# Probabilities of one attention head turned by DMA in 16-bit planes, and its products with V three slots later

## The chip, the cores and the metric

One core of a Trainium2 chip. The metric is the device time of one execution in microseconds. Engines are named as in the profile: PE is TensorE (PEld its weight loads), DVE is VectorE, ACT is ScalarE, POOL is GpSimd, SP is SyncE, which here only issues DMAs. L639 is line 639 of the kernel before.

## The reference

One encoder layer over 512 tokens of width 2048: a projection, two attention mixers of 8 heads each, an output projection, and a gated feed-forward part. The change is in the second mixer ("B"), which in the kernel is one masked softmax a head:

```
sc  = einsum('nbqhd,nbkhd->nbhqk', qb, kwin)
sc  = where(valid, sc, -inf)            # three dilated windows, merged by their denominators
lse = logsumexp(sc);  p = exp(sc - lse)
o   = einsum('nbhqk,nbkhd->nbqhd', p, vwin)
...
mixed = concatenate([rmsnorm(A), rmsnorm(B)]);  x = x + einsum('bse,ed->bsd', mixed, w_out)
```

## The kernel before, in words

**Products.** Every fp32 product is three passes (`mm3`, L229 to L231): both operands are split into a high part, written by ACT, and the remainder, written by DVE (`split`, L220 and L221). So each operand that a matmul takes has passed ACT and then DVE.

**Order.** All work is issued by one Python loop over weight units. A unit of the output projection is 12 matmuls of 128x512 (four row blocks, three passes each). Between units, and in the middle of most, a share of the side queue is issued: `give` pops tasks until its credit is used up. `drain_until` pops tasks until something is there that the next unit needs; reloading a parked head's output (`Back.load`, "oback") drains until that head's `oT` has been issued. The order on each engine is fixed when the program is built, and each engine takes its instructions in that order.

**Attention slots.** `head_slot(s)` issues what is due in slot s. A head has four blocks of 128 queries, so 16 heads take 64 slots and some more. In this document **slot 0 is the first score block of head B5**, the sixth head of the second kind; B5's scores are in slots 0 to 3, those of B6 in 4 to 7, those of B7 in 8 to 11. In its slots a block goes through:

- the score (`mm3`) into a PSUM bank, and at once the mask and row maximum on DVE (L639, an instruction that the profile calls CUSTOM_DVE_ANT_0, writing `p`), then the exponential on ACT (L649);
- one slot later the division by the row sum on DVE (L653, L654);
- `pt` (`TURN_LAG` = 5 slots after the first score): four PE transposes (L659) of one 128-column block of the four `p` tiles into a PSUM bank, then split into `pTh` (ACT) and `pTl` (DVE);
- `pv` (`VALUE_LAG` = 6): the product with V, three matmuls on `pTh`, `pTl`, `pTh`; after the last block `fin` copies the sum out (`oT`) and squares it.

**Turning by DMA.** q and k of later heads are already turned without PE, by the class `Turned`: `part` writes the low and the high 16 bits of the fp32 words as two planes ("plane", ACT, L551), `turn` transposes them by DMA ("words", SP, L556), `merge` interleaves them again ("merged", ACT, L561). The result is split like any operand (L220 to L224).

**Neighbours.** In the same stretch ACT and DVE split the weights ("arena" or "w" from "raw", L302 and L307), the reloaded outputs ("arena" from "oback", L1171 and L1175) and V of the next head ("arena" from "vraw"), and DVE adds finished banks of the output projection to x (L1195). PE can reuse those banks only after L1195.

Of the kernel before, what the change touches and what calls it, by code (L numbers as in the profile page):

```python
# [24 lines left out]
NT = S // P  # L25
# [37 lines left out]
TURN_LAG = 5  # L63
HEADS_HELD = 4
ROWS_AT = (6, 8, 10, 12, 14, 16, 19, 22, 25, 28)
VALUE_LAG = 6
COLUMN_BLOCKS = 3
SUM_LEAD = 6
ATTEND_PAST = 4
TURNED_ON_PE = {"A": 2, "B": 4}  # L70


def f32(ap):
    return ap.bitcast(F32)
# [3 lines left out]
def encoder_block(ctx, tc, x, w_in, g_q_a, g_k_a, w_out, w_gate_up, w_down, g_final, x_t, gains, c_ident, c_mask,  # L78
# [11 lines left out]
    def nm(base):  # L90
        counter[0] += 1
        return f"{base}_{counter[0]}"

    def slot(base, dtype=F32, shape=(P, 512)):
        return sp.tile(list(shape), dtype, tag="s", name=nm(base))
# [19 lines left out]
    def small(n=4):  # L115
        used[0] += n
        assert used[0] <= 512
        return fixed[:, used[0] - n:used[0]]
# [47 lines left out]
    def place(m, i):  # L166
        return form_tile(m, i).rearrange("p a b -> p (a b)")
# [46 lines left out]
    def split(src, name, gain=None, at=None):  # L214
        if at is None:
            hi, lo = slot(name + "h", F32R), slot(name + "l", F32R)
        else:
            hi, lo = (place(*h) for h in at)
        if gain is None:
            nc.scalar.activation(hi, src, AF.Copy)  # L220
            nc.vector.tensor_tensor(lo, src, f32(hi), op=OP.subtract)  # L221
        else:
            nc.scalar.activation(hi, src, AF.Copy, scale=gain)
            nc.vector.scalar_tensor_tensor(lo, src, gain, f32(hi), op0=OP.mult, op1=OP.subtract)  # L224
        return hi, lo
# [13 lines left out]
    class Pair:  # L239
        def __init__(self):  # L240
            self.parts = [sp.tile([P, 512], F32R, tag="tw", bufs=2 * TWINS, name=nm("tw")) for _ in range(2)]

        def __getitem__(self, at):
            return self.parts[at[1]]
# [252 lines left out]
    def reload(name, dst):  # L497
        assert stored[name] == NT, name
        whole = slot(name, F32, (P, NT, 512))
        nc.sync.dma_start(whole, spill[name].rearrange("t p c -> p t c"))  # L500
        dst.update((t, whole[:, t]) for t in range(NT))
        dst["whole"] = whole
# [68 lines left out]
    heads = []  # L571
    of_head = [small(12) for _ in range(HEADS_HELD)]

    class Head:
        def __init__(self, kind, h):
            self.kind, self.h = kind, h
            self.p, self.o = {}, None
            self.negm, self.z, self.rz = None, None, None

        def by_dma(self):  # L580
            return self.h >= TURNED_ON_PE[self.kind]

# [118 lines left out]
    def head_at(slot):  # L701
        h, i = divmod(slot, NT)
        return (heads[h], i) if 0 <= h < len(heads) else (None, i)

    def head_slot(s):
        def at(lag, f, only=None):
            head, i = head_at(s - lag)
            if head and (only is None or i == only):
                f(head, i)
        at(VALUE_LAG + 1, lambda head, i: head.add_squares(), NT - 1)  # L710
        at(0, Head.score)
        at(1, Head.norm)
        at(TURN_LAG, Head.pt)
        at(0, Head.exp)
        at(VALUE_LAG, Head.pv)
        at(VALUE_LAG, lambda head, i: head.fin(), NT - 1)

        def begin(lag, kind, f, dma=True):
            at(lag, lambda head, i: f(head) if head.kind == kind and head.by_dma() == dma else None, 0)
        begin(-4, "A", Head.tq, False)  # L720
        begin(-4, "B", Head.tq, False)
        for kind in "AB":
            begin(-2, kind, Head.tk, False)
        begin(-2, "A", Head.split_q)
        begin(-2, "A", Head.split_k)
        begin(-3, "A", Head.merge_q)
        begin(-3, "B", Head.split_q)
        begin(-4, "B", Head.merge_q)
        begin(-2, "B", Head.split_k)
        begin(-3, "B", Head.merge_k)  # L730
# [5 lines left out]
    def light(cost, tasks):  # L736
        return [weighed(cost, f) for f in tasks]

    def attention_tasks():
# [20 lines left out]
        def at(slot, tasks):  # L760
            extra.setdefault(slot, []).extend(tasks)
# [12 lines left out]
        for j in range(4):  # L774
            s = NT * (NHA + 2 * j)
            if 2 * j < TURNED_ON_PE["B"]:
                at(s - 11, light(0.1, [lambda j=j: reload(f"qkB{j}", qkB[j])]))
# [10 lines left out]
        for s in range(2 * NHA * NT + VALUE_LAG + 2):  # L788
            cost = 1.5 if s < NHA * NT else 1.2 if s < 2 * NHA * NT else 0.7
            todo += [weighed(cost, lambda s=s: head_slot(s))] + extra.get(s, [])  # L790
# [474 lines left out]
    for kind in "AB":  # L1265
        for c in range(NC):
            out_chunk(kind, c)
        if kind == "A":
            attend.append(len(units) + ATTEND_PAST)
    attend[1] += ATTEND_PAST  # L1270

# [279 lines left out]
    at = [0.0]  # L1551
# [147 lines left out]
```

## Time and profile before

| | |
|---|---|
| time, median of 3 runs | 1949.36 us (1949.17 to 1949.64) |
| the profiled execution's own time | 1947.76 us |
| its span, first to last instruction | 1946.0 us |
| busy share of the span | PE 99%, PEld 82%, DVE 79%, ACT 59%, POOL 7% |
| DMA | 413.50 MB, mean 212 GB/s |

The span is what the trace covers; 1.76 us of the execution lie around it. A busy share is a mean over stages; the stretch of the change runs from about 536 to 600 us.

### The profile page before, as it was taken

To read this page: it belongs to the slowest core of one execution; us is meant where nothing else is said; L and a number is where in the kernel's file an instruction comes from. 1 tells how busy PE (TensorE), PEld (TensorE's weight loads), DVE (VectorE), ACT (ScalarE), POOL (GpSimd) and SP (SyncE) were. 2 spreads that over 40 slices of the span, in tenths; PEclk is the share of its full clock that TensorE was granted. 3 is DMA by queue.
4 is the path that set the end of the run, shared out by engine and by line. 5 is a ranking of instruction groups with operands and counts; after the bars stand their busy time and mean duration, and the time that the engine had idled before them with its cause. 6 is when DMAs were issued, how large, how long until landed. Compare 5 with 4: busy or idle time off the path is not lost.

```text
span 1946.0 us, 24535 instructions
## 1 busy us (share of the span) xinstructions
PE 1932.1 (99%) x8687; PEld 1593.4 (82%) x8687; DVE 1537.4 (79%) x2020; ACT 1152.7 (59%) x1673; POOL 140.6 (7%) x184
## 2 busy tenths in 40 slices
PE   9999999999999999999999999999999999999998
PEld 7888887888888888888888888888888888888886
DVE  7987768888785697778778778787788978787886
ACT  7755556675765565555555555555555666555555
POOL 1000011000000000000000000000000121111121
PEclk9999999999999999999999999999999999999999
DMA  9676694354442556858658768678587798868865
GB/s 347 235 263 225 216 290 118 92 184 146 124 147 98 174 196 204 284 144 286 241 164 284 225 195 285 196 231 296 145 283 269 215 243 266 230 162 243 239 146 168
DMA packets 268924, 413.50 MB, mean 212 GB/s; under 512 B 75584, under 2 KB 102720, under 8 KB 268672
## 3 DMA queue, kind: packets, MB, share of 16 engines
q1 hardware_dynamic: 237968, 325.31, 51.6%
q0 software_dynamic: 22480, 60.57, 12.4%
q10 hardware_dynamic: 8352, 26.05, 4.1%
q8 instruction: 68, 1.11, 0.2%
q14 instruction: 56, 0.46, 0.1%
HBM read 334.52 MB, written 62.65 MB: 204 GB/s over the span
## 4 chain that ended last, share of the span: by engine, by line
PE 94%; DVE 3%; ACT 2%; issue 1%; DMA 0%; ACTq 0%; DVEq 0%; POOLq 0%; POOL 0%; SPq 0%
PE b L229 31%; PE b L231 30%; PE b L230 30%; PE b L659 1%; ACT rj L448 0%; DVE x L1195 0%; PE b L1241 0%; DVE w L307 0%; DVE ra L461 0%; ACT w L302 0%; DVE tw L966 0%; DVE qA L464 0%; DVE qA L470 0%; DMA stage<-in_w_in_dram 0%; DVE fixed L635 0%
## 5 line engine op out<-in xcount | busy, mean ns | idle before, releaser
L907 ACT ACTIVATE wide<-raw 128x1024 fp32r<-128x1024 f32 x462 | 487.1, 1058 | 457.6 <-PE b L231 269.6
L910 DVE TENSOR_TENSOR wide<-raw,wide 128x1024 fp32r<-128x1024 f32 x462 | 562.8, 1223 | 202.8 <-ACT wide L907 191.5
L229 PE MATMUL b<-wide,arena 128*128 128x512 f32 x1848 | 719.8, 390 | 0.0
L231 PE MATMUL b<-wide,arena 128*128 128x512 f32 x1848 | 719.2, 389 | 0.0
L230 PE MATMUL b<-wide,arena 128*128 128x512 f32 x1848 | 719.1, 389 | 0.0
L231 PEld LDWEIGHTS b<-wide,arena 128*128 128x128 f32 x1848 | 346.9, 188 | 72.3
L230 PEld LDWEIGHTS b<-wide,arena 128*128 128x128 f32 x1848 | 346.9, 188 | 71.7
L229 PEld LDWEIGHTS b<-wide,arena 128*128 128x128 f32 x1848 | 346.9, 188 | 71.7
L1043 DVE TENSOR_TENSOR raw<-raw,raw 128x1024 f32<-128x1024 f32 x264 | 321.6, 1220 | 7.0 <-DMA raw<-in_w_gate_up_dram 7.0
L230 PE MATMUL b<-tw,arena 128*128 128x512 f32 x396 | 154.3, 390 | 0.6 <-DVE tw L966 0.6
L231 PE MATMUL b<-tw,arena 128*128 128x512 f32 x396 | 154.2, 389 | 0.0
L229 PE MATMUL b<-tw,arena 128*128 128x512 f32 x396 | 154.1, 389 | 0.0
L963 ACT ACTIVATE tw<-stage 128x512 fp32r<-128x512 f32 x140 | 85.5, 629 | 69.3 <-DVE stage L1043 45.9
L966 DVE TENSOR_TENSOR tw<-stage,tw 128x512 fp32r<-128x512 f32 x140 | 93.9, 688 | 22.1 <-ACT tw L963 15.9
L229 PE MATMUL b<-w,arena 128*128 128x512 f32 x240 | 95.2, 397 | 0.0
L231 PE MATMUL b<-w,arena 128*128 128x512 f32 x240 | 93.9, 391 | 0.0
L230 PE MATMUL b<-w,arena 128*128 128x512 f32 x240 | 93.5, 390 | 0.0
L230 PEld LDWEIGHTS b<-tw,arena 128*128 128x128 f32 x396 | 74.3, 188 | 16.7 <-DVE tw L966 1.4
L231 PEld LDWEIGHTS b<-tw,arena 128*128 128x128 f32 x396 | 74.3, 188 | 15.9 <-DVE arena L354 0.4
L229 PEld LDWEIGHTS b<-tw,arena 128*128 128x128 f32 x396 | 74.3, 188 | 15.5
L380 DVE TENSOR_TENSOR pair<-pair 128x256 f32<-128x256 f32 x120 | 46.4, 423 | 46.7 <-ACT pair L1244 23.2
L220 ACT ACTIVATE pTh<-b 128x512 fp32r<-128x512 f32 x64 | 38.3, 598 | 64.4 <-PE b L659 62.5
(243 smaller groups left out, 2118.1 us busy)
## 6 DMA issues: line engine op xcount, KB each, us to landing
raw<-in_w_gate_up_dram SPq DMA_DIRECT2D x308, 512.0 KB, 6.3
raw<-in_w_down_dram SPq DMA_DIRECT2D x88, 512.0 KB, 7.4
stage<-in_w_in_dram SPq DMA_DIRECT2D x111, 256.0 KB, 5.4
forms<-pair POOLq DMA_DIRECT2D x22, 896.0 KB, 6.3
fr<-forms ACTq DMA_DIRECT2D x35, 512.0 KB, 5.3
raw<-in_w_out_dram SPq DMA_DIRECT2D x32, 512.0 KB, 4.2
x1d<-s POOLq DMA_DIRECT2D x54, 256.0 KB, 6.5
stage<-in_w_in_dram SPq DMA_DIRECT2D x90, 128.0 KB, 3.6
```

Source lines behind the costliest of these rows:

```text
L220: nc.scalar.activation(hi, src, AF.Copy)
L229: nc.tensor.matmul(dst, ah, bh, start=start, stop=False, skip_group_check=chained)
L230: nc.tensor.matmul(dst, ah, bl, start=False, stop=False, skip_group_check=chained)
L231: nc.tensor.matmul(dst, al, bh, start=False, stop=stop, skip_group_check=chained)
L380: nc.vector.tensor_tensor(out, x, y, op=op)
L659: nc.tensor.transpose(ps[:, t * P:(t + 1) * P], self.p[t][:, kb * P:(kb + 1) * P], ident)
L907: nc.scalar.activation(self.hi, self.src, AF.Copy)
L910: nc.vector.tensor_tensor(self.lo, self.src, f32(self.hi), op=OP.subtract)
L963: nc.scalar.activation(self.pair[:, 0], self.src, AF.Copy)
L966: nc.vector.tensor_tensor(self.pair[:, 1], self.src, f32(self.pair[:, 0]), op=OP.subtract)
L1043: nc.vector.tensor_tensor(t[dst], t[src[0]], t[src[1]], op=OP.add if form == "m6" else OP.subtract)
```

## The change

The probabilities of head B5 alone go through the DMA transpose: their planes are written in slots 2 to 5 and turned in slots 3 to 6, merged and split in slots 8 to 11, and multiplied with V in slots 9 to 12 (before: transposed in slots 5 to 8, multiplied in slots 6 to 9). `fin` and the sum of squares of B5 move from slots 9 and 10 to 12 and 13. Lines of the kernel after are 2 higher up to the class `Turned` and 24 to 31 higher below it: L221 becomes L223, L551 L553, L561 L563, L639 L663, L1195 L1226.

```diff
+P_BY_DMA = (('B', 5),)
+P_LAG = 3
...
+    class Rows:
+        def __init__(self, tiles):
+            self.tiles = tiles
+
+        def __getitem__(self, at):
+            return self.tiles.pop(at[1])
+
...
+        def p_by_dma(self):
+            return (self.kind, self.h) in P_BY_DMA
+
+        def p_part(self, t):
+            if t == 0:
+                self.turned_p = Turned(lambda: Rows(self.p))
+            self.turned_p.part(t)
+
+        def p_turn(self, t):
+            self.turned_p.turn(t)
+
+        def p_merge(self, kb):
+            self.pTs = getattr(self, "pTs", {})
+            self.pTs[kb] = split(self.turned_p.merge(kb), "pT")
...
-        at(VALUE_LAG + 1, lambda head, i: head.add_squares(), NT - 1)
+        def either(lag, f, dma, only=None):
+            at(lag, lambda head, i: f(head, i) if head.p_by_dma() == dma else None, only)
+        for late, dma in ((P_LAG, True), (0, False)):
+            either(VALUE_LAG + late + 1, lambda head, i: head.add_squares(), dma, NT - 1)
         at(0, Head.score)
         at(1, Head.norm)
-        at(TURN_LAG, Head.pt)
+        either(TURN_LAG, Head.pt, False)
         at(0, Head.exp)
-        at(VALUE_LAG, Head.pv)
-        at(VALUE_LAG, lambda head, i: head.fin(), NT - 1)
+        either(2, Head.p_part, True)
+        either(3, Head.p_turn, True)
+        either(TURN_LAG + P_LAG, Head.p_merge, True)
+        for late, dma in ((P_LAG, True), (0, False)):
+            either(VALUE_LAG + late, Head.pv, dma)
+            either(VALUE_LAG + late, lambda head, i: head.fin(), dma, NT - 1)
```

**ACT, slot 2.** Before; `p_4754` is B5's third exponential, `merged_4738` is k of head B6, whose high part goes to the arena:

```order
L220 ACTIVATE pTh_4762<-b_76 128x512
L649 ACTIVATE p_4754,fixed<-p_4754,fixed 128x512
L220 ACTIVATE arena_85<-merged_4738 128x512
L302 ACTIVATE arena_84<-raw_4496 128x512
L220 ACTIVATE pTh_4806<-b_75 128x512
```

The same place now:

```order
L222 ACTIVATE pTh_4762<-b_76 128x512
L673 ACTIVATE p_4754,fixed<-p_4754,fixed 128x512
L553 ACTIVATE plane_4767<-p_4670 128x1024
L222 ACTIVATE arena_85<-merged_4738 128x512
L304 ACTIVATE arena_84<-raw_4496 128x512
L222 ACTIVATE pTh_4808<-b_75 128x512
```

The first plane of B5's probabilities stands ahead of the high part of k.

**DVE, from the division in slot 9 to the mask of slot 10.** Before; `x_403` is x of the output projection:

```order
L654 TENSOR_SCALAR p_4994<-p_4994,fixed 128x512
L221 TENSOR_TENSOR pTl_5052<-b_75,pTh_5051 128x512
L307 TENSOR_TENSOR w_5023<-raw_4740,w_5022 128x512
L1175 SCALAR_TENSOR_TENSOR arena_85<-oback_4978,fixed,arena_85 128x512
L1195 SCALAR_TENSOR_TENSOR x_403_4784<-b_71,fixed,x_403_4784 128x512
L1195 SCALAR_TENSOR_TENSOR x_403_4784<-b_77,fixed,x_403_4784 128x512
L688 TENSOR_TENSOR acc_4217<-acc_4217,sq_5062 128x512
L639 ISA p_5092,fixed<-b_74,mask 128x512
```

And now:

```order
L678 TENSOR_SCALAR p_4977<-p_4977,fixed 128x512
L223 TENSOR_TENSOR pTl_5030<-b_73,pTh_5029 128x512
L223 TENSOR_TENSOR pTl_5037<-merged_5034,pTh_5036 128x512
L309 TENSOR_TENSOR w_5001<-raw_4740,w_5000 128x512
L1206 SCALAR_TENSOR_TENSOR arena_85<-oback_4961,fixed,arena_85 128x512
L1226 SCALAR_TENSOR_TENSOR x_404_4786<-b_71,fixed,x_404_4786 128x512
L1226 SCALAR_TENSOR_TENSOR x_404_4786<-b_77,fixed,x_404_4786 128x512
L663 ISA p_5070,fixed<-b_75,mask 128x512
```

The remainder of the merged block of B5 (`pTl_5037`) is new and stands ahead of four other instructions and of the next mask. ACT's order in the same slot of the kernel after shows what that remainder waits for (`p_5021` is the exponential of slot 9, whose mask is one slot up in DVE's order):

```order
L222 ACTIVATE pTh_5029<-b_73 128x512
L673 ACTIVATE p_5021,fixed<-p_5021,fixed 128x512
L563 ACTIVATE merged_5034<-words_4815 128x1024
L222 ACTIVATE pTh_5036<-merged_5034 128x512
L304 ACTIVATE w_5049<-raw_4826 128x512
```

The merge and its high part come behind the exponential of the same slot.

**PE, from the last transpose of slot 11 to slot 12.** Before; `b_78` is the bank of B6's output, `w` are weight units:

```order
L659 MATMUL b_74<-fixed,p_4960 128x128
L229 MATMUL b_78<-pTh_5100,arena_85 128x512
L230 MATMUL b_78<-pTl_5101,arena_85 128x512
L231 MATMUL b_78<-pTh_5100,arena_85 128x512
L229 MATMUL b_76<-w_5022,arena_85 128x512
L230 MATMUL b_76<-w_5023,arena_85 128x512
L231 MATMUL b_76<-w_5022,arena_85 128x512
L229 MATMUL b_75<-w_5022,arena_85 128x512
L230 MATMUL b_75<-w_5023,arena_85 128x512
L231 MATMUL b_75<-w_5022,arena_85 128x512
L659 MATMUL b_72<-fixed,p_4833 128x128
L659 MATMUL b_72<-fixed,p_4876 128x128
```

Now, with `b_76` the bank of B5's output and `b_78` that of B6's:

```order
L683 MATMUL b_72<-fixed,p_4954 128x128
L231 MATMUL b_76<-pTh_5085,arena_85 128x512
L232 MATMUL b_76<-pTl_5086,arena_85 128x512
L233 MATMUL b_76<-pTh_5085,arena_85 128x512
L231 MATMUL b_78<-pTh_5078,arena_85 128x512
L232 MATMUL b_78<-pTl_5079,arena_85 128x512
L233 MATMUL b_78<-pTh_5078,arena_85 128x512
L683 MATMUL b_75<-fixed,p_4839 128x128
L683 MATMUL b_75<-fixed,p_4885 128x128
L683 MATMUL b_75<-fixed,p_4925 128x128
L683 MATMUL b_75<-fixed,p_4954 128x128
L231 MATMUL b_76<-pTh_5135,arena_85 128x512
```

Slot 12 follows slot 11 with no weight matmul between: the reload of B5's output drains the side queue until B5's `fin`, which is now in slot 12. In slots 10 to 12 the products of B5 stand ahead of those of B6.

## Rows read from the trace of the kernel before

**Rows 1.** The page: the chain that ended last, share of the span by engine.

```profile
PE 94%; DVE 3%; ACT 2%; issue 1%; DMA 0%; ACTq 0%; DVEq 0%; POOLq 0%; POOL 0%; SPq 0%
```

**Rows 2.** Busy time from 563 to 581 us: PE, PEld, DVE, ACT, POOL, PEclk.

```profile
563.00:581.00 18.00, 18.00 (x89) 14.86 (x88) 16.20 (x36) 11.69 (x24) 0.54 (x1) 1.00 0.38 128
```

**Rows 3.** All waits of PE from 520 to 600 us: total, times, longest.

```profile
PE b L659 <- DVE x L1195: 0.6, 1, 0.6
```

**Rows 4.** Timeline of PE around slot 10: start, us, engine, line.

```profile
572.70 0.39 PE L231 MATMUL b<-arena 128*128 128x512 f32 x1
572.93 0.60 PE L659 MATMUL b<-fixed,p 128*128 128x128 f32 x4
...
574.07 0.40 PE L229 MATMUL b<-w,arena 128*128 128x512 f32 x1
...
576.82 0.39 PE L229 MATMUL b<-arena 128*128 128x512 f32 x1
```

**Rows 5.** The chain that ended last, in slots 2 and 3: start, us, what.

```profile
537.61 0.53 ACT arena L220
...
538.77 0.76 DVE x L1195
...
539.58 0.66 PE b L659 x4
```

**Rows 6.** Timeline of ACT with a merge and a plane of q and k.

```profile
515.20 1.18 ACT L561 ACTIVATE merged<-words 128x1024 uint16<-128x1024 uint16 x1
516.27 1.06 ACT L551 ACTIVATE plane<-qkB 128x1024 uint16<-128x1024 uint16 x1
517.22 0.63 ACT L302 ACTIVATE arena<-raw 128x512 fp32r<-128x512 f32 x1
```

**Rows 7.** All that writes or reads "words": duration ns min/median/max; last row the DMAs.

```profile
L556 SPq DMA_TRANSPOSE words<-plane x16: 1232/1250/2371, 323.0 to 517.4; - x16
...
DMA to landing us min/median/max: 3.0/3.1/6.1
```

**Rows 8.** All that writes or reads "merged": DVE's remainder of k.

```profile
L221 DVE TENSOR_TENSOR arena<-merged,arena x4: 692/693/693, 500.5 to 557.5; 128x512 fp32r<-128x512 f32 x4
```

**Rows 9.** Timeline of DVE in slot 5, up to the mask of slot 6.

```profile
550.32 0.69 DVE L639 CUSTOM_DVE_ANT_0 p<-b,mask 128x512 f32<-128x512 f32 x1 [1.28 <-PE b L231]
...
551.53 0.69 DVE L221 TENSOR_TENSOR pTl<-b,pTh 128x512 fp32r<-128x512 f32 x1
553.58 0.69 DVE L224 SCALAR_TENSOR_TENSOR arena<-merged,arena 128x512 fp32r<-128x512 f32 x1 [1.36 <-ACT arena L223]
...
555.39 0.68 DVE L639 CUSTOM_DVE_ANT_0 p<-b,mask 128x512 f32<-128x512 f32 x1
```

**Rows 10.** Timeline of ACT in slots 5 and 6.

```profile
551.25 0.71 ACT L649 ACTIVATE p<-p,fixed 128x512 f32<-128x512 f32 x1
...
556.12 0.73 ACT L649 ACTIVATE p<-p,fixed 128x512 f32<-128x512 f32 x1 [0.21 <-DVE fixed L639]
...
556.84 0.61 ACT L220 ACTIVATE arena<-merged 128x512 fp32r<-128x512 f32 x1
```

**Rows 11.** Timeline of DVE in slot 8, up to the mask of slot 9.

```profile
562.64 0.69 DVE L639 CUSTOM_DVE_ANT_0 p<-b,mask 128x512 f32<-128x512 f32 x1 [0.70 <-PE b L231]
...
565.54 0.69 DVE L307 TENSOR_TENSOR w<-raw,w 128x512 fp32r<-128x512 f32 x1
566.14 0.75 DVE L1175 SCALAR_TENSOR_TENSOR arena<-oback,fixed,arena 128x512 fp32r<-128x512 f32 x1
566.80 0.75 DVE L1195 SCALAR_TENSOR_TENSOR x<-b,fixed,x 128x512 f32<-128x512 f32 x1
...
568.57 0.69 DVE L639 CUSTOM_DVE_ANT_0 p<-b,mask 128x512 f32<-128x512 f32 x1
```

**Rows 12.** DMA issues: tiles, queue, operation, count, KB each, us to landing.

```profile
oB<-oT POOLq DMA_DIRECT2D x6, 256.0 KB, 2.6
oback<-oB SPq DMA_DIRECT2D x6, 256.0 KB, 3.0
```

## The prediction

> **What bounds the kernel now.** I read the page first. The chain that ended last is 94% PE [rows 1], so a stretch is worth what it adds to or takes from PE. Then the list of PE's waits around the change: from 520 to 600 us there is one, 0.6 us, for DVE's L1195 [rows 3]. In the second half of that stretch PE is busy for 18.00 of 18 us at clock 1.00, DVE for 16.20 and ACT for 11.69 [rows 2]: DVE has 10% left, ACT 35%. So PE has no slack; whatever DVE hands over late is paid in full. Last I read the timelines, to see in what order ACT and DVE hand over. The reader is to see there that both engines take their queues in order: a DVE row in slot 5 stands idle for 1.36 us for a high part that ACT has not yet written, and what is queued behind it stands with it [rows 9].
>
> **Removed.** Sixteen PE transposes. A group of four starts 0.23 us after the last score matmul, and the first weight matmul, behind three product matmuls, 1.14 us after the group, of which the three take 0.69 at 0.229 each (12 matmuls are 2.75) [rows 4]: a group costs 0.45 us, four groups 1.8 us. All of it is on PE's path. The twelve product matmuls only move.
>
> The Trainium skill, page "VectorE: DVE Perf Modes", section "The three transpose paths", prices one 128x128 bf16 transpose at 390 ns on TensorE and 1309 ns through the DMA crossbar, and its table of rules takes TensorE wherever a PSUM destination is good enough. By that figure, 16 transposes would give back an estimated 6.2 us and the sum below would be +1.5; the row says 1.8, since transposes follow each other in a pipeline, and I take the row.
>
> **Added on ACT.** Four planes: 0.95 us each from start to next start. Four merges: 1.07 us each [rows 6]. The four high parts stay, now read from SBUF as k's is, 0.61 us each [rows 10]. That is 8.1 us more over slots 2 to 11, some 40 us in which ACT idles for about a third [rows 2]; the sum fits, so the question is only where it stands in the queue.
>
> **Added on DMA.** Four transposes on SP, 1.25 us to issue (2.37 at most) and 3.1 us to landing (6.1 at most) [rows 7]. The last plane is written in slot 5 and first read in slot 8, and the masks of these slots start 12 us apart [rows 9, 11], so I cost them at nothing; what hides them is the three slots of lag, and with a lag of one they would be on the path. The loads behind them on SP (V of B6, the first reloaded output) are issued in slot 6 instead of earlier and read in slots 7 and 8, with 3.0 us to landing [rows 12]; I cost them at nothing too.
>
> **Slot 3, sure loss.** The one wait of PE in this stretch comes from a chain without slack: ACT's high part of B6's k at 537.61, DVE's remainder, L1195 at 538.77, then PE at 539.58 [rows 5]. The first plane now stands directly ahead of that high part. It delays all of it by 0.95 us, and PE is already waiting: **+0.95 us**.
>
> **Slots 5 to 8, lateness builds up.** With that 0.95 the mask of slot 5 starts at 551.27. Its exponential starts 0.73 later, at 552.00, where it was 551.25 before [rows 9, 10]; then comes the last plane, 0.95, then as before `oT`, the square and the high part of q. So DVE gets that high part at 555.28, not 553.58: 1.70 later. It waits for it in order, and the mask of slot 6 moves from 555.39 to 557.09 [rows 9]. From there: exponential 557.82 and 0.72 long, high part of k 558.54 and 0.61 long [rows 10], so DVE at 559.17, its remainder and a weight remainder 0.60 each, mask of slot 7 at 560.4; with 1.21 for mask and division [rows 9] and another remainder, mask of slot 8 at 562.2. PE finishes that score sooner than before: 562.6 before [rows 11], + 0.95, less three groups (1.35) and two moved products (six matmuls, 1.38), 560.8. So this mask starts 1.4 us late. Nothing on PE waits for it yet.
>
> **Slots 8 to 12, the loop.** Each of these slots has a ring through the two queues that was not there before. The mask releases the exponential; the merge stands behind the exponential on ACT; the high part follows the merge; DVE's new remainder waits for that high part and stands ahead of the next mask. Before, the high part came from a PE transpose ahead of the exponential, so the ring was open. One turn is 0.73 + 0.72 + 1.07 + 0.64 + 0.60 = 3.8 us (the 0.60 is DVE's pitch for the remainder, 0.69 long), plus what stands between remainder and mask on DVE: a weight remainder 0.60, an output remainder 0.66, and in two of the three slots two L1195 of together 1.4 (0.75 each, overlapping), in one also V's remainder, 0.60 [rows 6, 8, 10, 11]. That makes 7.0 (slot 8 to 9), 6.4 (9 to 10), 5.0 us (10 to 11). From the mask of slot 11 to the end of the last remainder of B5 it is another 3.9 (0.73, 0.72, 1.07, 0.64 and the 0.69). Sum 22.3: PE can have B5's last low part at 562.2 + 22.3 = 584.5.
>
> PE alone would reach the second matmul of that product earlier. From the end of slot 8's score it has 42 weight matmuls, 9 of scores and 15 of products up to there, at 0.229 each 15.1 us, and four groups of transposes (B6's), 1.8, together 16.9 us: 560.8 + 16.9 = 577.7. **The ring costs PE 584.5 - 577.7 = 6.8 us**, in steps: slot 10's low part is there at 562.2 + 7.0 + 3.9 = 573.1, where PE would be at 570.9 (40 matmuls and two groups on), 2.2 us; slot 11's 6.4 later, at 579.5, where PE would be at 576.1, 3.4 us in all; the other 3.4 in slot 12. Slots 11 and 12 stand with no weight matmul between them, because the reload of B5's output drains to B5's `fin`; that takes away the cover that 6 matmuls would give there. In slots 10 to 12 B5's products stand ahead of B6's, so PE cannot use the wait for them. Behind slot 12 the ring is open again, and the rest of the program has no wait that would swallow a shift.
>
> **What lies around the end.** B5's output is parked and reloaded, 2.6 + 3.0 us [rows 12] and the issues between. Before the unit that uses it stand four others, 48 matmuls or 11 us. ACT's instruction for it stands ahead of a high part of B7's second block, which PE needs some 9 us after that `fin`, an estimate of 0.4 us to spare by the same rows. I cost it at nothing.
>
> **Sum.** -1.8 + 0.95 + 6.8 = +5.95 us against the profiled execution: 1947.76 + 5.95 = 1953.7 (a span of 1946.0 + 5.95, and the 1.76 around it). That execution is 1.6 us below the median of the runs; on the median, 1949.36 + 5.95 = **1955.3**. Every operation added has rows of its own shape; what no row shows is how the ring closes. Its bounds: with slot 8's mask on time 5.4 instead of 6.8, and with pitches shorter by 0.1 a turn 5.0; with the longest rows, and a transpose that lands after 6.1 us where 3.1 was counted, 8.5. The likeliest case's own range is so 1953.5 to 1957.
>
> **Rivals.** Differences under 0.2% (3.9 us) a measurement of this kernel cannot tell from no change.
>
> - *The lag covers all* (the other side: not slower). The ring does not hold PE, because ACT, idle for 35% of the stretch, catches up inside each slot. For it: the merge could run any time after slot 6, and three lag slots were left. Against it: ACT takes its queue in order. It decides at the turn: if a turn is below PE's own 4.6 to 5.2 us a slot, nothing is lost. Then -1.8 + 0.95 = -0.85: 1948.5. Chance 0.08.
> - *Half a ring.* Masks 6 to 8 come on time, and PE's waits overlap with what it does anyway, so the ring costs 1.5 to 4.7: total +0.65 to +3.85, in the middle 1951.6. For it: all terms are small differences of long sums. Chance 0.2.
> - *A second wait behind it.* The reload of B5's output lands late (as a transpose once took 6.1 us where 3.1 is usual [rows 7]) and holds ACT ahead of B7's high part: 3.0 us late less the 0.4 of margin, +2.6, with the ring +8.55: 1957.9. It decides at that margin. Chance 0.1.
> - *The transposes were dearer than their group.* If each group cost all of the 1.14 us up to the weight matmul [rows 4], PE would gain 4.6 us and the sum be +3.15: 1952.5. Against it: the three products between take their 0.69 in any case. Chance 0.04. The skill's 390 ns would lead further that way, to the +1.5 above.
> - *The gain without any loss* is -1.8, within the bound, so faster by over 0.2% needs a mechanism that I don't see: 0.02.
>
> **Numbers.** The forecast (+4 to +7.6) has 0.56 left. Slower by over 0.2%: the forecast and the late reload, 0.66. Within 0.2%: half ring, covering lag and dearer transposes, 0.32. Faster: 0.02. The range cuts off the covering lag and the outer ends of the half ring and of the late reload: 1950.8 to 1958.2.
>
> **What would show it.** In the profile after, PE waits in slot 3 for DVE's L1226 1.5 us instead of 0.6; PE waits for the remainder `pTl` (L223) in slots 10, 11 and 12, together 6 to 7 us; DVE's masks of slots 9 to 11 start 3 to 6 us behind their scores, with 6.4 and 5.0 us between them; 16 fewer transposes, and ACT busy for 8 to 9 us more. The prediction is wrong if the masks start with their scores, if PE waits for ACT or a DMA instead, or if waits appear outside 536 to 600 us.

## The result and the profile after

The changed kernel takes 1956.66 us, median of 5 runs (1955.8 to 1958.17), the kernel before, beside it on the same chip, 1949.64 us (1949.17 to 1950.03): ratio 1.004 [1.003, 1.0051], 7.0 us slower by the medians. The forecast was 1955.3 us, range 1950.8 to 1958.2.

Medians are too coarse for the terms of the sum. Of 33 runs of the kernel before beside the second set of experiments, 11 lay between 1947.65 and 1948.35 us and 22 between 1949.19 and 1950.32: two groups, 1.6 us apart by their means. The profiled run of before belongs to the lower one, that of after starts late: all that POOL does from 50 us on stands 1.7 us later, long before B5. I therefore price the change by two POOL rows, one ahead of the stretch and one behind it. Timeline of POOL (start, duration), kernel before:

```profile
494.69 0.54 POOL L679 DMA_DIRECT2D oB<-oT  x1 [20.14 <-ACT oT L676]
868.73 0.91 POOL L1345 DMA_DIRECT2D forms<-pair  x1 [55.37 <-DVE pair L380]
```

The same two in the kernel after:

```profile
496.39 0.54 POOL L703 DMA_DIRECT2D oB<-oT  x1 [20.12 <-ACT oT L700]
878.32 0.92 POOL L1376 DMA_DIRECT2D forms<-pair  x1 [55.71 <-DVE pair L382]
```

868.73 - 494.69 = 374.04 us before, 878.32 - 496.39 = 381.93 after. **The change costs 7.89 us in its stretch**; the sum of the prediction was 5.95. Below, this difference against 374.04 is called the stage cost of a kernel. It comes from one profiled execution of each kernel; the runs of one changed kernel lie 1.6 to 5.2 us apart, so a difference of a few tenths between two stage costs is a reading of two traces and not a measured mean.

On the page after, busy time and chain:

```profile
PE 1936.7 (99%) x8671; PEld 1595.3 (82%) x8671; DVE 1536.5 (79%) x2020; ACT 1161.0 (59%) x1681; POOL 141.0 (7%) x184
...
PE 92%; DVE 4%; ACT 2%; issue 1%; DMA 1%; DVEq 0%; SPq 0%; POOLq 0%; POOL 0%; ACTq 0%
```

Against [rows 1], PE's share of the chain falls from 94% to 92%. All waits of PE from 538 to 602 us after (total, times, longest), where [rows 3] had one of 0.6:

```profile
PE b L231 <- ACT pTh L222: 3.7, 2, 1.9
PE b L683 <- DVE x L1226: 1.5, 1, 1.5
PE b L232 <- DVE pTl L223: 0.2, 1, 0.2
```

The wait for L1226 stands in slot 3, as forecast. Those for high part and remainder stand in slots 10 and 12; in slot 11 PE has none. Timeline of DVE after, the masks of slots 8 to 11 and B5's four remainders:

```profile
564.00 0.68 DVE L663 CUSTOM_DVE_ANT_0 p<-b,mask 128x512 f32<-128x512 f32 x1
...
567.34 0.69 DVE L223 TENSOR_TENSOR pTl<-merged,pTh 128x512 fp32r<-128x512 f32 x1 [2.05 <-ACT pTh L222]
...
571.14 0.68 DVE L663 CUSTOM_DVE_ANT_0 p<-b,mask 128x512 f32<-128x512 f32 x1
...
574.43 0.69 DVE L223 TENSOR_TENSOR pTl<-merged,pTh 128x512 fp32r<-128x512 f32 x1 [1.41 <-ACT pTh L222]
...
577.62 0.68 DVE L663 CUSTOM_DVE_ANT_0 p<-b,mask 128x512 f32<-128x512 f32 x1
...
580.93 0.69 DVE L223 TENSOR_TENSOR pTl<-merged,pTh 128x512 fp32r<-128x512 f32 x1 [1.42 <-ACT pTh L222]
...
582.80 0.69 DVE L663 CUSTOM_DVE_ANT_0 p<-b,mask 128x512 f32<-128x512 f32 x1
...
586.10 0.69 DVE L223 TENSOR_TENSOR pTl<-merged,pTh 128x512 fp32r<-128x512 f32 x1 [1.41 <-ACT pTh L222]
```

This is the ring: DVE stands idle ahead of each remainder, for 2.05 us in slot 8 and 1.41 or 1.42 in the other three, and the mask behind it is late; 7.14, 6.48 and 5.18 us from mask to mask, where 7.0, 6.4 and 5.0 were forecast. ACT's part of one turn, between the mask at 571.14 and the remainder at 574.43 (timeline of ACT after):

```profile
571.86 0.72 ACT L673 ACTIVATE p<-p,fixed 128x512 f32<-128x512 f32 x1 [2.41 <-DVE fixed L663]
...
572.58 1.16 ACT L563 ACTIVATE merged<-words 128x1024 uint16<-128x1024 uint16 x1
573.77 0.63 ACT L222 ACTIVATE pTh<-merged 128x512 fp32r<-128x512 f32 x1
```

ACT itself stands idle for 2.41 us for that mask, with a merge in its queue whose data are there: the last transpose was issued at 555.57 and took 6.2 us at most to land. PE's side of it was not forecast whole. Timeline of PE after, slots 10 to 12, and behind it the busy time in stretches (PE, PEld, DVE, ACT, POOL, granted clock):

```profile
574.45 0.50 PE L231 MATMUL b<-pTh,arena 128*128 128x512 f32 x1 [1.77 <-ACT pTh L222]
575.17 0.50 PE L232 MATMUL b<-pTl,arena 128*128 128x512 f32 x1 [0.22 <-DVE pTl L223]
...
577.14 0.63 PE L232 MATMUL b<-w,arena 128*128 128x512 f32 x1
577.57 0.63 PE L233 MATMUL b<-w,arena 128*128 128x512 f32 x1
...
586.12 0.62 PE L231 MATMUL b<-pTh,arena 128*128 128x512 f32 x1 [1.91 <-ACT pTh L222]
586.84 0.80 PE L232 MATMUL b<-pTl,arena 128*128 128x512 f32 x1
```

```profile
572.00:576.00 4.00, 2.00 (x11) 1.24 (x9) 2.59 (x5) 3.97 (x7) 0.00 (x0) 1.00 0.00 0
576.00:580.00 4.00, 4.00 (x12) 3.14 (x11) 3.47 (x8) 1.67 (x4) 0.00 (x0) 0.57 0.22 66
580.00:584.00 4.00, 3.91 (x22) 2.92 (x20) 3.04 (x7) 3.07 (x6) 0.00 (x0) 1.00 0.27 75
584.00:586.00 2.00, 0.20 (x2) 0.00 (x0) 0.69 (x2) 1.97 (x5) 0.00 (x0) 1.00 0.67 243
586.00:590.00 4.00, 3.78 (x9) 2.72 (x10) 3.11 (x6) 2.44 (x6) 0.54 (x1) 0.57 0.01 4
```

Behind each of the two stalls the granted clock is at half, the 1.2 GHz level: 0.50 from 576.10 to 579.51 and from 586.34 to 589.75 us, so 0.57 as the mean of the two stretches of 4 us. They hold twelve and nine matmuls where a full stretch has 22, and the matmuls start 0.43 us apart (577.14, 577.57) instead of 0.23.

### The profile page after: what moved, and what is told of

The parts are those of the page before. It is cut to its first block, busy times and chain, and to the rows that moved or that the text cites. A ratio compares the mean times of both kernels' runs of the same rounds, so it can differ in the third digit from the quotient of the medians.

```text
span 1955.3 us, 24531 instructions
## 1 busy us (share of the span) xinstructions
PE 1936.7 (99%) x8671; PEld 1595.3 (82%) x8671; DVE 1536.5 (79%) x2020; ACT 1161.0 (59%) x1681; POOL 141.0 (7%) x184
## 4 chain that ended last, share of the span: by engine, by line
PE 92%; DVE 4%; ACT 2%; issue 1%; DMA 1%; DVEq 0%; SPq 0%; POOLq 0%; POOL 0%; ACTq 0%
PE b L231 30%; PE b L232 30%; PE b L233 30%; PE b L683 1%; DVE x L1226 1%; DMA raw<-in_w_in_dram 0%; PE b L1272 0%; DVE w L309 0%; ACT rj L450 0%; ACT p L673 0%; DVE p L663 0%; PE b L891 0%; ACT merged L563 0%; DVE ra L463 0%; DVE tw L997 0%
## 5 line engine op out<-in xcount | busy, mean ns | idle before, releaser
L1376 POOL DMA_DIRECT2D forms<-pair x22 | 20.1, 913 | 777.1 <-DVE pair L382 751.2
```

The costliest lines, as they stand in the source:

```text
L1376: nc.gpsimd.dma_start(forms_dram[:, :, n], hpart[0][:, 256:].rearrange("p (f c) -> p f c", c=256))
```

## The experiments

The theory: what the change costs is a ring through two in-order queues (mask, exponential, merge, high part, remainder, next mask), and the plane ahead of k's high part in slot 3; behind the stalls the clock falls. The rivals: ACT's 8 us of added work, wherever it stands; late data; a lag that is too short.

| kernel | median, us | ratio, 95% | row ahead | row behind | stage cost |
|---|---|---|---|---|---|
| changed | 1956.66 | 1.004 [1.003, 1.0051] | 496.39 | 878.32 | +7.89 |
| transposes left out | 1946.85 | 0.9992 [0.9984, 1.0001] | 495.07 | 867.18 | -1.93 |
| merge ahead | 1950.57 | 1.0009 [1.0, 1.0018] | 494.84 | 870.34 | +1.46 |
| planes late | 1955.55 | 1.0033 [1.0021, 1.0046] | 496.11 | 876.60 | +6.45 |
| PE filled | 1955.9 | 1.0036 [1.0023, 1.0048] | 496.11 | 876.80 | +6.65 |
| both edits | 1948.81 | 0.9999 [0.999, 1.0008] | 495.01 | 868.86 | -0.19 |
| both, lag 2 | 1949.74 | 1.0004 [0.9995, 1.0013] | 494.93 | 870.15 | +1.18 |
| head B6 | 1951.21 | 1.0014 [1.0006, 1.0023] | 495.29 | 870.10 | +0.77 |
| both, head B4 | 1948.31 | 0.9995 [0.9986, 1.0004] | 496.09 | 868.71 | -1.42 |
| merge first | 1953.85 | 1.0026 [1.0017, 1.0036] | 494.88 | 873.30 | +4.38 |
| both, B4 and B5 | 1952.9 | 1.002 [1.0011, 1.0029] | 497.12 | 874.18 | +3.02 |

The kernel before, beside them: 1949.64 us with the changed kernel, 1949.51 with the four below it, 1949.36 with the next four, 1949.38 with the last two. Line numbers below are each kernel's own.

**The transposes alone.** With no head by DMA the order is that of the kernel before; the transposes of B5 are left out:

```diff
-P_BY_DMA = (('B', 5),)
+P_BY_DMA = ()
+P_UNTURNED = (('B', 5),)
...
         def pt(self, kb):
+            if (self.kind, self.h) in P_UNTURNED:
+                self.pTs = getattr(self, "pTs", {})
+                self.pTs[kb] = split(self.p[kb], "pT")
+                return
```

> The slots of the kernel before, but the probabilities of B5 go untransposed from SBUF into the split (the transposition of this head is left out, nothing takes its place). It prices the gain alone. Theory: 0.45 us for each of four groups of transposes, so 1.8 us less than the kernel before, ratio about 0.999. Rival (the transposes were dearer than their group): 1.14 us each, 4.6 us less, ratio 0.9977.

Stage cost -1.93 us, 0.48 a group. The transposes are worth what the row of the trace said, not 1.14 a group. The trace does not agree with the 6.2 us that the prediction estimated from the Trainium skill's page "VectorE: DVE Perf Modes", section "The three transpose paths". So the most that the change can gain is 1.9 us.

**The merge ahead of the exponential.**

```diff
-        either(TURN_LAG, Head.pt, False)
+        either(TURN_LAG + P_LAG, Head.p_merge, True)
+        either(TURN_LAG, Head.pt, False)
         at(0, Head.exp)
         either(2, Head.p_part, True)
         either(3, Head.p_turn, True)
-        either(TURN_LAG + P_LAG, Head.p_merge, True)
```

> The changed kernel with merge and split of B5 issued ahead of the exponential of their slot instead of behind it. Theory (a ring of mask, exponential, merge, high part, remainder, next mask): the ring is open, PE has no wait in slots 10 to 12, the masks of slots 9 to 11 start with their scores, the clock stays at 1.00, and what is left is -1.8 for the transposes and +0.95 in slot 3: 0.5 to 1 us below the kernel before, 8 to 9 us below the changed one. Rival (ACT's added load of 8 us, or data that the DMA brings late, hold PE wherever the merge stands): the waits stay at 4 us or more, and the time at 3 us or more above the kernel before.

From +7.89 to +1.46, with the same instructions in number and kind, the same DMAs and the same lag: load, data and lag are out as the main cause, the order in the two queues, ACT's above all, is it. The clock stays at 1.00. But the waits are not all gone (timeline of PE):

```profile
571.45 0.50 PE L232 MATMUL b<-pTl,arena 128*128 128x512 f32 x1 [0.52 <-DVE pTl L223]
...
577.04 0.66 PE L683 MATMUL b<-fixed,p 128*128 128x128 f32 x4 [0.71 <-DVE pTl L223]
...
580.14 0.50 PE L232 MATMUL b<-pTl,arena 128*128 128x512 f32 x1 [0.31 <-DVE pTl L223]
```

Now DVE is what is late, and it is full (PE, PEld, DVE, ACT):

```profile
570.00:574.00 4.00, 3.48 (x18) 2.54 (x17) 3.96 (x10) 3.74 (x7) 0.00 (x0) 1.00 0.00 1
574.00:578.00 4.00, 3.29 (x18) 2.42 (x17) 3.96 (x9) 3.19 (x6) 0.00 (x0) 1.00 0.55 158
```

The lag has put B5's remainders into the slots that have B6's already. I had forecast -0.5 to -1 here and not counted that.

**The planes last in their slot.**

```diff
-        either(2, Head.p_part, True)
...
         begin(-3, "B", Head.merge_k)
+        either(2, Head.p_part, True)
```

> The changed kernel with the planes issued last in their slot, behind the splits of the next head's q and k. Theory: PE's wait in slot 3 is 0.6 us again instead of 1.5, the masks of slots 6 to 8 are on time, and the ring stays: PE waits in slots 10 to 12, and the clock falls behind the waits. Time 0.95 to 2.4 us below the changed kernel, 5.5 to 7 above the one before. Rival (slot 3 waits for ACT's load, wherever the plane stands): the wait stays at 1.5 and the time at that of the changed kernel.

The wait in slot 3 is back at 0.6, and slot 8's mask at 561.82 is, with the start taken off (561.82 - 1.42 against 564.00 - 1.70), 1.9 us earlier than in the changed kernel. The ring stays: the masks of slots 8 to 11 are 7.34, 6.49 and 5.17 us apart. All waits of PE from 520 to 610 us, and two stretches (PE, PEld, DVE, ACT, POOL, granted clock):

```profile
PE b L231 <- ACT pTh L222: 3.9, 3, 1.9
PE b L232 <- DVE pTl L223: 0.7, 3, 0.2
PE b L683 <- DVE x L1226: 0.6, 1, 0.6
PE b L683 <- DVE fixed L663: 0.4, 1, 0.4
```

```profile
574.00:578.00 4.00, 4.00 (x20) 3.27 (x19) 3.49 (x8) 1.67 (x4) 0.00 (x0) 1.00 0.24 66
...
584.00:588.00 4.00, 3.63 (x10) 2.68 (x11) 3.11 (x6) 2.94 (x7) 0.54 (x1) 0.74 0.09 31
```

Stage cost +6.45, 1.44 less than the changed kernel: 0.94 of it is slot 3. The clock did not fall behind every stall, which I had expected: behind slot 10's, 1.47 us, it stays at 1.00, and it falls only behind slot 12's, 1.92 us.

**PE filled with zeros.** The computation is unchanged: what is added to B5's product is zero.

```diff
+FILL = (0, 8, 5, 8)
...
+            if self.p_by_dma():
...
+                for _ in range(FILL[kb]):
+                    nc.tensor.matmul(self.o, self.zero, vB[self.h][0], start=False, stop=False)
             mm3(self.o, v, self.pTs.pop(kb), kb == 0, kb == NT - 1)
```

> The changed kernel with 21 more matmuls by a tile of zeros into the bank of B5's product, ahead of the products that wait: 8, 5 and 8 in slots 10, 11 and 12, 0.229 us each. PE then works instead of waiting 1.8 to 2 us. Theory (the granted clock fell because PE stood idle, and the fall cost 1.5 us twice, a part of it hidden): clock 1.00 from 572 to 600 us, masks and remainders as in the changed kernel, time about 2 us below the changed kernel, although PE does 4.8 us more work. Rival (the clock falls in this stretch for another reason, or its fall costs nothing since the ring sets the pace): the clock falls as before, or the time is that of the changed kernel or up to 1 us above.

In the stretches in which the changed kernel had 0.57:

```profile
576.00:580.00 4.00, 4.00 (x22) 3.30 (x20) 3.21 (x8) 1.89 (x3) 0.00 (x0) 1.00 0.25 73
...
586.00:590.00 4.00, 3.78 (x18) 2.87 (x19) 2.96 (x6) 2.93 (x7) 0.54 (x1) 1.00 0.13 49
```

The clock stays up, and the masks stand where they stood (slot 11's at 582.54 - 1.42 = 581.12, against 582.80 - 1.70 = 581.10). Stage cost +6.65: PE does 21 matmuls more, and the stretch is 1.24 us shorter. So with the idleness the fall of the clock went too, and it had cost some 1.2 us by these two traces, not the 2 that I expected. The runs alone, 1955.9 against 1956.66, lie too close to show it. A reason for the small price: the first of the two falls lies in slot 11, where PE would have waited for the ring in any case; with the planes late, where the clock stays up there, it waits 0.50 us for the high part and 0.23 for the remainder.

**Both edits together.** Merge ahead and planes last.

> The two edits together: merge and split of B5 ahead of the exponential, the planes last in their slot. Theory: the two losses are separate, so both go: PE's wait in slot 3 is 0.6 us, the masks of slots 6 to 8 are on time, and of the waits for DVE in slots 10 to 12 (1.5 us with the merge ahead alone, there with the mask of slot 8 still 1.4 us late) most go too. 0 to 1.5 us below the kernel before. Rival (DVE has too much in slots 9 to 11, where two heads' remainders stand in one slot, and is late there whenever slot 8 starts): the waits stay at 1 us or more, and the time is the same as before or up to 1 us above.

Stage cost -0.19: the losses are separate, and add (6.43 and 1.44 alone, 8.08 together). Of the 1.9 that the transposes are worth 1.74 is still lost; the waits for remainders, 1.0 us by the profile, are the part that the trace names, and they are for DVE (waits of PE from 480 to 620 us, of which 0.6 for L1226 was there before):

```profile
PE b L683 <- DVE x L1226: 1.2, 2, 0.6
PE b L683 <- DVE pTl L223: 0.7, 1, 0.7
PE b L232 <- DVE pTl L223: 0.3, 1, 0.3
```

(The second wait for L1226 lies near 502 us, and the kernel before has it there too.) By the runs it is the same as the kernel before.

**Both edits, a lag of two.** `P_LAG = 2`.

> As with both edits, and a lag of two slots instead of three: merges in slots 7 to 10, products in 8 to 11. Theory (DVE is full where two heads' remainders stand in one slot, and with two slots of lag that are two slots instead of three): the waits for DVE fall under 0.5 us, the time is 1 to 2 us below the kernel before. Rival (the last transpose, issued in slot 6, has not landed when its merge is due in slot 7): ACT waits for the DMA in slot 7, and PE behind it, the time above that of a lag of three.

The rival. Timeline of ACT in slot 7, and further on in the drain:

```profile
558.96 1.19 ACT L563 ACTIVATE merged<-words 128x1024 uint16<-128x1024 uint16 x1 [0.85 <-DMA words<-plane]
...
586.44 0.72 ACT L1202 ACTIVATE arena<-oback,fixed 128x512 fp32r<-128x512 f32 x1 [3.79 <-DMA oback<-oB]
```

The first merge waits 0.85 us for its transpose; PE waits 0.79 us behind it. ACT's instruction for the reload of B5's output now stands ahead of the copy of B6's output, while the reload is issued no earlier than with both edits at a lag of three (583.67 and 583.30): it holds ACT for 3.79 us instead of 1.69, and PE for 0.71 behind that. So three slots of lag do cover the DMA, and two do not. The theory had a part of the truth: PE's waits for remainders fell from 1.0 to 0.5 us.

**The changed code, at head B6.** `P_BY_DMA = (('B', 6),)`, nothing else.

> The changed kernel's code as it is, but for head B6 instead of B5: its merges stand in slots 12 to 15, behind the last mask (that of slot 11). Theory (the loss is a ring through the next mask): no ring, so PE does not wait for high part and remainder by 1.8 us at a time; what can be left is ACT, which there has 3.6 us of work a slot for PE's 3.1, so waits of 0.5 us in each of three slots, and up to 1 us for the planes. Time from 1.8 us below the kernel before to 1.5 above. Rival (merges and planes cost PE by their load on ACT, wherever they stand): 5 to 8 us above the kernel before, as with B5.

Stage cost +0.77 instead of +7.89, by the same planes, merges and splits. All waits of PE from 545 to 610 us:

```profile
PE b L231 <- ACT pTh L222: 1.2, 2, 1.0
PE b L232 <- DVE pTl L223: 0.5, 2, 0.2
```

With no mask behind the merges there is no ring. But the profiled run is the fastest of eleven, 1949.75 us; four of the others took 1953.36 to 1954.97, up to 5.6 above the kernel before. No trace shows what they lost, so the +0.77 holds for the profiled execution, and the rival of the load is not excluded in those.

**Both edits, at head B4.** `P_BY_DMA = (('B', 4),)`.

> Both edits (merge ahead of the exponential, planes last), for head B4 instead of B5: planes in slots -2 to 1, merges in slots 4 to 7. There one remainder of B5 stands in each of the three later slots, as B6's did behind B5's. Theory: the same gain without the same loss, 0 to 1.5 us below the kernel before, nearly as with B5. Rival (the gain depends on the room that a head's neighbourhood leaves on DVE, and here slots 2 and 5, where PE waited or DVE waited for ACT already, leave none): above the kernel before.

Stage cost -1.42, the best of all; one wait of PE has come, 0.5 us for a remainder, and one of the two for L1226 (0.6 each) has gone. By the runs 0.9995 [0.9986, 1.0004]: below what a measurement of this kernel tells from no change.

**The merge ahead of the whole slot.** The line of `p_merge` moved above `at(0, Head.score)`.

> The changed kernel with merge and split of B5 ahead of everything of their slot, so that the merge stands ahead of the exponential but the remainder ahead of the mask. Theory (the ring counts by what stands in series in the two queues): a shorter ring is closed again, through the mask of the same slot: mask 0.73, exponential 0.72, one or two splits 0.5 each and an output 0.6, merge 1.2, high part 0.65, remainder 0.6, next mask: 5.5 us from slot 8 to 9, then 5.0 and 5.0. The last remainder is there 3 us late, and the time is 2 to 3.5 us above the kernel before, 1 to 2 above that with the merge beside the other head's transposes. Rival (all that counts is that the merge stands ahead of the exponential): the same time as there within 0.4 us, and masks of slots 9 to 11 that start with their scores.

Timeline of DVE, the masks of slots 8 to 11:

```profile
565.75 0.68 DVE L663 CUSTOM_DVE_ANT_0 p<-b,mask 128x512 f32<-128x512 f32 x1
...
571.64 0.68 DVE L663 CUSTOM_DVE_ANT_0 p<-b,mask 128x512 f32<-128x512 f32 x1
...
576.70 0.68 DVE L663 CUSTOM_DVE_ANT_0 p<-b,mask 128x512 f32<-128x512 f32 x1
...
581.75 0.68 DVE L663 CUSTOM_DVE_ANT_0 p<-b,mask 128x512 f32<-128x512 f32 x1
```

Turns of 5.89, 5.06 and 5.05 us where 5.5, 5.0 and 5.0 were worked out: the ring is closed again, although the merge stands ahead of the exponential. It shows as idle time of DVE ahead of the first and the last remainder, 2.56 and 1.29 us. Ahead of the two between there is none: there DVE's other work takes as long as the ring. Stage cost +4.38, above my 2 to 3.5: I had counted PE's waits for remainders, and here PE also waits for a mask (1.8 us) and for a division (1.0), since the masks themselves are behind the ring.

**More heads.** B2 and B4, B4 and B5, and B2, B4, A3, A5 and A7, each with both edits.

> Both edits, for heads B2 and B4 together; two heads apart, so that the planes, merges and products of one end before those of the other begin. Theory: B4 alone gave 1.4 us in the stretch, twice that is 2.8: 2 to 3 us below the kernel before. Rival (B2, whose neighbours still turn q and k on PE, leaves less room): 0.5 to 1.5 below.

> Both edits, for B4 and B5 together, whose slots overlap: B4's merges stand beside B5's planes. Theory (what the two give alone adds up: -1.4 and -0.2): 1.6 us below the kernel before. Rival (planes and merges in the same slots fill ACT's queue, so the high parts come late as with the changed kernel): 1 us or more above it.

> Both edits, for B2 and B4 and for A3, A5 and A7 of the first mixer, in whose stage the projections run beside the heads. Theory (the gain is the transposes' 0.45 us a group wherever PE is never waited for): 1.4 us a head, 7 us below the kernel before. Rival (in the first mixer ACT reads the score from PSUM and its queue is what PE waits for): the two B heads give 2.8 and the A heads take it back, the time is that of the kernel before or above.

All three miss. B2 with B4: 1951.28 us, 1.0009 [1.0, 1.0018], stage cost +1.41 (from 495.31 to 870.76). In front of B4 the trace shows PE waits of 1.1 us for a high part and 1.5 for a remainder near 508 and 521 us; B2's merges stand there among the planes and merges of q and k of the next pair, all on ACT. B4 with B5: 1952.9, stage cost +3.02 instead of -1.6; PE waits 2.6 us for high parts, three of the four times where B4's merges stand beside B5's planes. With the three A heads: 1966.78 us, 1.0089 [1.0076, 1.0103]. From 390 to 480 us ACT is busy for 27.68, 25.65 and 23.85 of 30 us and PE for 27.30, 24.67 and 23.28, where the kernel before has PE at 29.97, 29.83 and 30.00. The clock falls there too, to 0.50 from 460.35 to 467.18 us. So the gains of single heads don't add. That ACT's queue is the cause in these three is not shown: no run tries it, and in the last the profile puts most of PE's waits down to DVE (4.7 us for remainders, 3.6 for divided rows).

## Why the prediction was right, and where it was off

The forecast of slower, its place and its mechanism held; 1956.66 lies in the range. Step by step:

- *Removed, 1.8 us.* Measured 1.93.
- *Slot 3, +0.95.* PE's wait there is 1.54 us instead of 0.60, +0.94; with the planes last it is 0.60 again.
- *Slots 5 to 8.* Masks of slots 5 to 8 forecast at 551.27, 557.09, 560.4 and 562.2, measured, less 1.70, at 551.29, 557.18, 560.49 and 562.30.
- *The ring, 6.8 us.* From the mask of slot 8 to the end of the last remainder 22.3 us were worked out, 22.79 measured (586.10 + 0.69 - 564.00). The difference is one number used four times: for the merge I took 1.07 us, its pitch to an instruction that doesn't read its result [rows 6]; to the high part, which does, it is 1.19 (572.58 to 573.77 above). Four times 0.12 is 0.5.
- *What PE does behind a stall, not in the sum.* The clock falls behind two of the stalls: 1.24 us, by the traces of the changed and the filled kernel.
- *DMA transposes and loads behind them, nothing.* Right: in the changed kernel no merge waits for a DMA. The lag of two shows that the cover ends there.
- *Reload of B5's output, nothing.* Right, barely: ACT waits 0.37 us for it, PE not at all.

5.95 + 0.5 + 1.24 = 7.7 of 7.89. So the term that was mis-sized is the ring's: 6.8 was forecast, and with the clock it is 7.89 + 1.93 - 0.94 = 8.9, of which 7.3 are the ring by its own rows, 1.24 the clock, and 0.3 are not assigned. 8.9 lies above the longest ring that was allowed for, 8.5, which had counted a transpose that lands late; no merge waited for one. On the median of before the stage cost gives 1949.36 + 7.89 = 1957.25, just above the likeliest case's own range of 1953.5 to 1957. That the measured median, 1956.66, lies inside it owes something to luck.

The signs came out in part. PE's wait in slot 3, 16 transposes fewer, 8.3 us more of ACT and no new wait of PE outside the stretch are there. PE's waits for B5's operands come to 3.9 us by the profile, not 6 to 7: behind the stalls PE worked at half the clock for 6.8 us in all, which is 3.4 us lost (an estimate from the two stretches) while the ring went on. They stand in slots 10 and 12 and not in 11, where the half clock took the place of the wait. And 3.7 of the 3.9 are for ACT's high part: to the letter that was a sign of being wrong. PE reads the high part ahead of the remainder, and both are steps of the same ring, so the mechanism stands, but the sign should have named both. The masks of slots 9 and 10 start 3.9 and 5.4 us behind the end of their scores, as forecast, that of slot 11 only 1.2, since PE's score was late there itself. The rivals "the lag covers all", "half a ring" and "dearer transposes" fell by these runs; "a second wait behind it" did not occur here, only with the lag of two.

That the slot 3 loss and the ring are the causes is shown, by undoing each and both. That DVE's fullness in slots 9 to 11 is all that keeps both edits from the full 1.9 is read from the trace, and not shown: the lag of two lowered these waits and brought others.

## What to carry to other kernels

Before an operation moves between engines that take their queues in order, write down for one period what waits for what, through both queues: a merge that stood a few instructions too far back cost 6.4 us of 7.9 here, while both engines stood idle for each other. Place such work so that its result is needed only by something at least one period away, and count a dependent step by the pitch between two instructions that depend on each other. The best use of the idea was worth 1.4 us of 1949 by its trace, since a group of four PE transposes between other matmuls costs 0.48 us here, and in three tries with more heads the gain did not multiply.

## What was not expected of the hardware

The granted clock fell to half for 3.4 us behind stalls of 1.77 and 1.91 us, though PE had been busy for 11.87 of the 12 us ahead of the first slot concerned, 560 to 572; with matmuls by zeros in the place of the stalls it stayed at 1.00. It doesn't follow each such wait: with the planes late it stayed at 1.00 behind 1.47 us, and in the kernel with the merge first PE waits 1.81 us for the mask ahead of 582.50, and the stretch around it and behind it shows 1.00 (PE, PEld, DVE, ACT, POOL, granted clock):

```profile
580.00:584.00 4.00, 2.19 (x12) 1.54 (x12) 2.79 (x8) 2.99 (x7) 0.00 (x0) 1.00 0.07 25
584.00:588.00 4.00, 4.00 (x21) 3.30 (x20) 3.44 (x7) 4.00 (x8) 0.54 (x1) 1.00 0.19 70
```

What decides it, these runs leave open. And the idle time that the profile gives for a wait of PE is less than what it costs: in the kernel with the merge ahead, the second matmul of slot 10's product starts 1.00 us after the first (570.45 to 571.45), without a wait in slot 9 it is 0.32 (565.89 to 566.21), so 0.68 us is lost where 0.52 is shown.
